# One matmul pair for both parts of the meta tokens, and the second half's factor row one unit earlier, in a hybrid attention and mLSTM encoder layer

## The chip, the cores and the metric

The kernel runs on one core of one Trainium2 chip. The metric is the device time of one execution in microseconds, taken over several runs; the median is compared. The kernel before was run three times: 2815.20, 2803.92 and 2798.67 us, median 2803.92 us.

## What is computed

One encoder layer is applied to two sequences, a prompt of 1024 tokens and a sample of 2048 tokens, each preceded by the same 16 learned "meta" tokens. Everything is in fp32.

```python
def _encoder_layer(h, g_pre, w_in, b_in, na_rpb, ml_conv_w, ml_head_g, w_a, w_b, w_out, g_post):
    xn = _rmsnorm(h, g_pre)
    proj = xn @ w_in + b_in
    na_q, na_k, na_v, na_z, ml_qk, ml_v, ml_z, ml_o, ml_g, mg = jnp.split(proj, SPLIT_IDX, axis=-1)
    ya = _neighbourhood_attention(na_q, na_k, na_v, na_rpb)
    ya = (ya * jax.nn.silu(na_z)) @ w_a
    yb = (_mlstm_branch(ml_qk, ml_v, ml_g, ml_o, ml_conv_w, ml_head_g) * jax.nn.silu(ml_z)) @ w_b
    ga, gb = jnp.split(jax.nn.sigmoid(mg), 2, axis=-1)
    y = (ga * ya + gb * yb) @ w_out
    return h + _rmsnorm(y, g_post)
```

`D_MODEL` is 1024 and the combined projection `w_in` has 6672 columns. The meta tokens take part in both mixers (their keys and values are seen by every attention query, and the mLSTM starts with them) and are dropped at the end.

## The kernel before, in words

**Split products.** Every operand of a large product is held as two parts, a high part in the rounded fp32r format and a low part that is the rest (`xh` and `xl` for the tokens, `whi` and `wlo` for the weights). A product is three matmuls added up in one PSUM bank: high by high, high by low, low by high. The product low by low is left out.

**Two streams.** `dense` is a Python generator that issues the projections and the closing products; `sparse` issues the two mixers. `run` takes from both in turns, by estimated TensorE costs that each `yield` hands over, so the order on TensorE is written out by hand. On the other engines and on SyncE, whose queue starts nearly all transfers, a planner orders the instructions by a simulated timeline.

**The dense stream.** `PLAN` lists groups of columns for pieces of 1024 tokens, which are treated as two halves of 512. The first group, (0, 0, "m"), is the mLSTM part for the whole prompt, the second, (0, 0, "n"), the attention part. Only these two compute the meta tokens, once for both sequences. While the first group runs, the sparse stream has nothing to do yet; the second runs beside the mLSTM of the prompt.

**Jobs of a group.** `layout` makes jobs of two kinds. A feature-major job ("fm", `fm_half`) has four units; a unit is 128 columns of the weights, as stationary operand, by 512 tokens (or two times 264, with the meta tokens, in the first half). A token-major job ("tm", `tm_unit`) has the tokens as the stationary operand, 128 at a time, and 256 or 264 weight columns as the moving operand; over the eight slices of the contraction that is 24 matmuls for each 128 tokens. The first group is one fm job, six tm jobs and a second fm job.

**The meta tokens in a tm job.** They are an entry of their own in the list `todo` (`tok` is None, 16 stationary columns). The order in a job is four times 128 tokens of the first half, then the meta tokens, then four times 128 of the second half. Five tm jobs have such an entry: the one with the columns from 4360 on (gates, 264 wide), two of the mLSTM values, and two of the attention values (256 wide). Each is 24 matmuls with 16 stationary columns (L590 to L592), one evacuation (L601: multiply by the token's norm factor `rc`, add the bias) and two small stores.

**PSUM.** There are three banks under the tag `pj`, two under `tr`, one under `sc`, two under `sm`. tm jobs use `pj` alone, so an entry needs the bank that was filled three entries earlier.

**The norm factor of the prompt.** For the prompt, `x` is not multiplied by its RMS factor ahead of the product; the factor is multiplied in at evacuation. In fm units it has to lie along the free axis, so `rrows` (L317 to L321) makes a row of it: a diagonal matrix times ones on TensorE (tag `sm`), copied by ScalarE into `rr`. Until `rr` exists, the first units of a half cannot be evacuated. `group` therefore gives the units banks from the list `("pj", "pj", "pj", "tr", "tr", "sc")` and collects their evacuations in `late`. When unit `lu` is done with its third quarter (`q == 2`), the function in `self.rwait` issues the row product; after unit `lu`, all evacuations collected are issued. `lu` is 2 in the first half, where a unit takes two banks, and 3, the last unit of the job, in the second half. After that job comes the first tm job, on `pj`.

**The opening.** `opening` loads the first tokens and weights, makes their high and low parts (ScalarE and VectorE by turns), and the factors of the first 512 tokens and of the meta tokens. The pool `xp`, on the right side of SBUF, holds its temporary tiles and is closed when the second half's row is issued; the pools of the mixers take that room afterwards.

**A chain across the group.** The gate columns of the tm job with 264 columns go to DRAM (`gg`, L627 and L629) and are read back as `g_t` (L956, L957) by the prompt's mLSTM, whose first instructions on ScalarE and VectorE are L965 and L966.

Of the kernel before, what the change touches and what calls it, by code (L numbers as in the profile page):

```python
# [9 lines left out]
F32 = mybir.dt.float32  # L10
F32R = mybir.dt.float32r
I32 = mybir.dt.int32
AF = mybir.ActivationFunctionType
ALU = mybir.AluOpType
# [3 lines left out]
P = 128  # L18
# [102 lines left out]
class K:  # L121
# [231 lines left out]
    def opening(self, xp):  # L353

        nc, wp, cp = self.nc, self.wp, self.cp
        self.gpre = cp.tile([P, KT], F32, name="gpre")
        nc.sync.dma_start(self.gpre, self.i["g_pre"])
        nc.vector.tensor_scalar(self.gpre, self.gpre, -0.125, None, op0=ALU.mult)
        xm = cp.tile([P, KT, NM], F32, name="xm")
        nc.sync.dma_start(xm, self.i["xm"].rearrange("p (k t) -> p k t", k=KT))  # L360
        xts = [self.xtload(0, 0, 0, xp, 9)]
        self.wload(1)
        xts += [self.xtload(0, 0, e, xp, 9) for e in (1, 2, 3)]
        self.wload(2)
        mt = xp.tile([P, D], F32, name="xr", bufs=9)
        nc.sync.dma_start(mt[:NM], self.i["meta"])
        toks = self.tokens(0, 0, (0, 1), xp, 9)
        self.wload(3)
        toks += self.tokens(0, 0, (2, 3), xp, 9)
        self.setup2()  # L370
        self.xnext = [self.xtload(0, 512, e, wp, 4) for e in (0, 1)]
        self.wload(4)
        self.xnext += [self.xtload(0, 512, e, wp, 4) for e in (2, 3)]
        self.toks = self.tokens(0, 512, range(4), xp, 9)
        x = self.xparts()
        self.xs.append(tuple(x))
        g = self.gpre.rearrange("p (k a) -> p k a", a=1).to_broadcast([P, KT, NM])
        nc.vector.tensor_tensor(xm, xm, g, op=ALU.mult)
        nc.scalar.activation(x[0][:, :, :NM], xm, AF.Copy)
        nc.vector.tensor_tensor(x[1][:, :, :NM], xm, x[0][:, :, :NM].bitcast(F32), op=ALU.subtract)  # L380
        for e in range(4):
            self.xsplit(x, xts[e], e, NM, self.gpre)
            if e == 0:
                self.wpump(1, 4)
        self.wpump(2, 2)
        self.wpump(3, 2, nc.vector.tensor_copy)
        res = []
        for _ in self.rsum(toks, res, (mt, NM)):
            pass
        self.rc = cp.tile([P, 9], F32, name="rc")  # L390
        self.rr = wp.tile([P, 2, 512], F32, name="rr", tag="gain", bufs=1)
        self.rm = cp.tile([P, NM], F32, name="rm")
        dt = wp.tile([P, HALF], F32, name="dt", tag="thT", bufs=1)
        dg, dm = self.rdiag(res[0], dt), dt[:NM, 512:]
        nc.vector.tensor_scalar(dm, self.ident[:NM, :NM], res[0][:NM, 4:5], None, op0=ALU.mult)
        nc.vector.tensor_copy(self.rc[:, 0:4], res[0][:, 0:4])
        nc.vector.tensor_copy(self.rc[:, 8:9], res[0][:, 4:5])
        self.wpump()
        self.wrp = wp, 2

        def rows():
            self.rrows(dg, self.rr[:, 0], "sm")
            p = self.psum("sm", [P, 512])
            nc.tensor.matmul(p[:, :NM], self.ones[:NM], dm, start=True, stop=True)
            nc.scalar.activation(self.rm, p[:, :NM], AF.Copy)
        self.rwait[0, 0] = rows
# [163 lines left out]
    def tm_unit(self, col, halves, wd):  # L570
        nc, wp = self.nc, self.wp
        ws = self.wtake(2)
        bb = wp.tile([P, WU], F32, name="bb", bufs=2)
        nc.sync.dma_start(bb[:, :wd], _bc(self.i["b_in"], col, wd))
        todo = []
        for x, s, t0, meta in halves:
            base = NM if meta else 0
            todo += [(x, s, base + 2 * P * j, P, 2, t0 + 2 * P * j) for j in range(2)]
            if meta and not (C_MZ <= col < C_GA - wd):
                todo.append((x, s, 0, NM, 1, None))  # L580
        for j, (x, s, c, n, cnt, tok) in enumerate(todo):
            st = wp.tile([P, 2, WU], F32, name="stT", bufs=4)
            for a in range(cnt):
                p = self.psum("pj", [P, 512])
                o = p[:n, :wd]
                xs = slice(c + a * P, c + a * P + n)
                for k in range(KT):
                    wh, wl = ws[k // 4][0][:, k % 4, :], ws[k // 4][1][:, k % 4, :]
                    xh, xl = x[0][:, k, xs], x[1][:, k, xs]
                    nc.tensor.matmul(o, xh, wh, start=k == 0, stop=False)  # L590
                    nc.tensor.matmul(o, xh, wl, start=False, stop=False)  # L591
                    nc.tensor.matmul(o, xl, wh, start=False, stop=k == KT - 1)  # L592
                    if k == 3:
                        if j == len(todo) - 1 and a == cnt - 1:
                            self.wdone()
                        yield 12 * C256
                if j == len(todo) - 1 and a == cnt - 1:
                    self.wdone()
                if s == 0:
                    r = 8 if tok is None else tok // P + a  # L600
                    nc.vector.scalar_tensor_tensor(st[:n, a, :wd], p[:n, :wd], self.rc[:n, r:r + 1], bb[:n, :wd], op0=ALU.mult, op1=ALU.add)  # L601
                else:
                    nc.vector.tensor_tensor(st[:n, a, :wd], p[:n, :wd], bb[:n, :wd], op=ALU.add)
                if a == cnt - 1:
                    self.tm_store(col, wd, s, n, cnt, tok, st)
                yield 12 * C256

    def tm_store(self, col, wd, s, n, cnt, tok, st):
        nc, wp = self.nc, self.wp
# [81 lines left out]
    def group(self, s, t0, meta, cols, reuse, nxt):  # L691
# [4 lines left out]
        for j, (kind, c) in enumerate(jobs):  # L696
            if kind == "tm":
                for cost in self.tm_unit(c[0], [(x,) + h for x, h in zip(self.xs, todo)], c[1]):
                    yield cost
                    self.beside()  # L700
                continue
            ws = self.wtake(len(c))
            last = j == len(jobs) - 1
            for hf in range(2):
                side = None
                if j == 0 and hf == 0 and not reuse:
                    side = self.spread(self.build_half(*todo[1][:2], self.xs), 15)
                elif last and nxt and nxt[0] == "f":
                    side = self.spread(self.ystart(*nxt[1:]), 15) if hf else None
                elif last and nxt:  # L710
                    if hf == 0:
                        nres = []
                        nb = self.build_half(*nxt[:2], nres)
                        side = self.spread(nb, 15, "scaled")
                    else:
                        side = self.spread(nb, 15)
                late = tags = None
                if todo[hf][:2] in self.rwait:
                    late = []
                    tags = iter(("pj", "pj", "pj", "tr", "tr", "sc"))  # L720
                    lu = 3 if hf else 2
                for u, (col, w) in enumerate(zip(c, ws)):
                    for q, cost in enumerate(self.fm_half(col, w, self.xs[hf], *todo[hf], done=self.wdone if hf else None, tags=tags, late=late)):
                        yield cost
                        if side:
                            side()
                        if self.fout:
                            next(self.fout, None)
                        self.beside()
                        if late is not None and u == lu and q == 2:  # L730
                            self.rwait[todo[hf][:2]]()
                    if late is not None and u == lu:
                        for evac in late:
                            evac()
                        late = tags = None
                        del self.rwait[todo[hf][:2]]
                if side:
                    side(True)
# [918 lines left out]
    def dense(self, ctx):  # L1657

        tc, nc = self.tc, self.nc
        self.wp = ctx.enter_context(tc.tile_pool(name="wp", bufs=1, reuse_waits="tile"))  # L1660
        self.requests()
        self.xp = ExitStack()
        xp = self.xp.enter_context(tc.tile_pool(name="xp", bufs=1, side="right", reuse_waits="tile"))
        self.wrp = xp, 4
# [23 lines left out]
    def sparse(self):  # L1688

        for kind, s, rts in STEPS:  # L1690
            if kind == "ml":
                for t0 in range(0, SEQLEN[s], 1024):
                    yield ("m", s, t0)
                yield from self.ml(s)
            else:
                types = _row_types(SEQLEN[s] // 64)
                for t0 in range(0, SEQLEN[s], 1024):
                    if any((types[b][1] + types[b][2]) * 64 > t0 for b in rts):
# [79 lines left out]
```

## Time and profile before

| | |
|---|---|
| median of three runs | 2803.92 us |
| lowest, highest | 2798.67, 2815.20 us |
| the profiled execution's own time | 2802.44 us |
| its span, first to last instruction | 2800.7 us |
| mean granted TensorE clock | 0.998 |
| VectorE, ScalarE busy | 65%, 47% of the span |
| HBM traffic | 233 GB/s over the span |

The profile's page gives the busy time of each engine, the chain of work that ended last, and groups of instructions with the tile they write and read, their count, busy time, mean duration, and the idle time of the engine ahead of them with what ended it. Matmuls are pipelined: one that is listed with 0.28 us is followed by the next after about 0.12 us, so durations of matmuls overlap and a sum of them is not a time. Spacing, from start to start, is what the engine spends. PE is the matmul side of TensorE, PEld its loading of stationary operands, DVE is VectorE, ACT is ScalarE, POOL is GpSimd, SPq is the queue of SyncE.

### The profile page before, as it was taken

Reading aid. Unit: us, or ns where it says so; the run is one execution under the profiler, and the core shown is the slowest. Engines: PE = TensorE matmul, PEld = TensorE weight load, DVE = VectorE, ACT = ScalarE, POOL = GpSimd, SP = SyncE. Lnnn points to the kernel's source line nnn. Section 1 sums busy time; section 2 is a strip of 40 time slices with the busy share of each in tenths; the row PEclk is TensorE's granted clock in tenths of the full one; section 3 lists DMA queues with packets and bytes.
Section 4 is the critical chain, followed back from the end, with each engine's and each line's share of the span. In section 5 each row is a group of like instructions: output and inputs, shape, how many; then the busy total and the mean of one; then the engine's idle time right before and its main releaser. Section 6 shows DMA issues by size and latency. Waiting matters only on the chain.

```text
span 2800.7 us, 48806 instructions
## 1 busy us (share of the span) xinstructions
PE 2766.8 (99%) x17120; PEld 2461.0 (88%) x17120; DVE 1827.2 (65%) x5075; ACT 1313.6 (47%) x3183; POOL 16.2 (1%) x103
## 2 busy tenths in 40 slices
PE   9999999999999999999999999999999999999998
PEld 7998898999899988988888888878887989889898
DVE  5232688676556655456768666575669888797954
ACT  5122556444444444355456555463455645545421
POOL 0000000000000000000000000000000000000000
PEclk9999999999999999999999999999999999999999
DMA  9555768755965554685666786565569898998965
GB/s 369 182 184 196 257 201 315 266 182 176 351 206 176 174 156 142 195 284 167 190 207 207 235 285 216 182 204 170 179 214 349 299 332 255 321 276 279 323 241 212
DMA packets 378278, 655.10 MB, mean 234 GB/s; under 512 B 50896, under 2 KB 199840, under 8 KB 378032
## 3 DMA queue, kind: packets, MB, share of 16 engines
q1 hardware_dynamic: 376912, 649.29, 70.2%
q0 software_dynamic: 1120, 2.69, 0.4%
q8 instruction: 135, 2.21, 0.3%
q14 instruction: 111, 0.91, 0.1%
HBM read 449.61 MB, written 202.22 MB: 233 GB/s over the span
## 4 chain that ended last, share of the span: by engine, by line
PE 88%; DMA 6%; DVE 4%; ACT 1%; issue 1%; SPq 0%; DVEq 0%; ACTq 0%
PE pj L169 15%; PE pj L170 15%; PE pj L171 15%; PE pj L590 7%; PE pj L591 7%; PE pj L592 7%; PE pj L1568 3%; PE sm L923 3%; PE pj L1570 3%; PE pj L1569 3%; PE tr L908 3%; DMA um<-ud 2%; DMA wlo<-wl 1%; PE sm L171 1%; PE sm L170 1%
## 5 line engine op out<-in xcount | busy, mean ns | idle before, releaser
L169 PE MATMUL pj<-xh,whi 128*128 128x512 f32 (+1 forms) x1792 | 705.4, 394 | 1.6 <-ACT whi L263 1.2
L170 PE MATMUL pj<-xl,whi 128*128 128x512 f32 (+1 forms) x1792 | 689.7, 385 | 0.1
L171 PE MATMUL pj<-xh,wlo 128*128 128x512 f32 (+1 forms) x1792 | 688.2, 384 | 0.2 <-DVE wlo L264 0.2
L590 PE MATMUL pj<-whi,xh 128*128 128x256 f32 (+3 forms) x1576 | 450.0, 286 | 1.5 <-ACT st L520 1.5
L591 PE MATMUL pj<-wlo,xh 128*128 128x256 f32 (+3 forms) x1576 | 444.4, 282 | 0.9 <-DMA wlo<-wl 0.9
L592 PE MATMUL pj<-whi,xl 128*128 128x256 f32 (+3 forms) x1576 | 444.3, 282 | 0.0
L171 PEld LDWEIGHTS pj<-xh,wlo 128*128 128x128 f32 x1792 | 337.2, 188 | 71.7 <-DVE wlo L264 0.4
L169 PEld LDWEIGHTS pj<-xh,whi 128*128 128x128 f32 x1792 | 337.2, 188 | 61.9 <-ACT whi L263 2.0
L170 PEld LDWEIGHTS pj<-xl,whi 128*128 128x128 f32 x1792 | 337.7, 188 | 57.3 <-issue 1.0
L590 PEld LDWEIGHTS pj<-whi,xh 128*128 128x128 f32 (+1 forms) x1576 | 294.3, 187 | 3.4 <-ACT st L520 1.9
L591 PEld LDWEIGHTS pj<-wlo,xh 128*128 128x128 f32 (+1 forms) x1576 | 293.9, 186 | 2.1 <-DMA wlo<-wl 1.1
L592 PEld LDWEIGHTS pj<-whi,xl 128*128 128x128 f32 (+1 forms) x1576 | 293.8, 186 | 0.9
L1568 PE MATMUL pj<-whi,mh 128*128 128x256 f32 x768 | 220.5, 287 | 3.1 <-DMA whi<-wh 3.1
L1570 PE MATMUL pj<-whi,mlo 128*128 128x256 f32 x768 | 216.5, 282 | 0.0
L1569 PE MATMUL pj<-wlo,mh 128*128 128x256 f32 x768 | 216.3, 282 | 0.0
L915 DVE TENSOR_TENSOR pts<-tr,pts 96x512 fp32r<-96x512 f32 (+2 forms) x192 | 131.8, 687 | 93.0 <-ACT pts L910 92.3
L910 ACT ACTIVATE pts<-tr 96x512 fp32r<-96x512 f32 (+2 forms) x192 | 113.9, 593 | 134.7 <-PE tr L908 134.4
L169 PE MATMUL pj<-yh,whi 128*128 128x512 f32 x384 | 154.5, 402 | 0.0
L171 PE MATMUL pj<-yh,wlo 128*128 128x512 f32 x384 | 151.3, 394 | 0.0
L170 PE MATMUL pj<-yl,whi 128*128 128x512 f32 x384 | 151.0, 393 | 0.0
L1568 PEld LDWEIGHTS pj<-whi,mh 128*128 128x128 f32 x768 | 145.3, 189 | 5.5 <-DMA whi<-wh 4.0
L1569 PEld LDWEIGHTS pj<-wlo,mh 128*128 128x128 f32 x768 | 145.5, 189 | 1.6
(283 smaller groups left out, 4991.4 us busy)
## 6 DMA issues: line engine op xcount, KB each, us to landing
whi<-wh SPq DMA_DIRECT2D x176, 512.0 KB
wlo<-wl SPq DMA_DIRECT2D x176, 512.0 KB
wraw<-wu SPq DMA_DIRECT2D x64, 512.0 KB
wh<-whi SPq DMA_DIRECT2D x64, 512.0 KB
wl<-wlo SPq DMA_DIRECT2D x64, 512.0 KB
gt<-st SPq DMA_DIRECT2D x96, 256.0 KB
tg<-gt SPq DMA_DIRECT2D x96, 256.0 KB
xt<-xt SPq DMA_DIRECT2D x32, 512.0 KB
```

The source lines that it names most:

```text
L169: mm(out, ah, bh, start=start, stop=False)
L170: mm(out, ah, bl, start=False, stop=False)
L171: mm(out, al, bh, start=False, stop=stop)
L590: nc.tensor.matmul(o, xh, wh, start=k == 0, stop=False)
L591: nc.tensor.matmul(o, xh, wl, start=False, stop=False)
L592: nc.tensor.matmul(o, xl, wh, start=False, stop=k == KT - 1)
L908: nc.tensor.transpose(pt[:ks, ch, :], pr_[:, ch * ks:(ch + 1) * ks], self.ident)
L910: nc.scalar.activation(pts[:ks, :, 0, :], pt[:ks], AF.Copy)
L915: self.nc.vector.tensor_tensor(pts[:ks, :, 1, :], pt[:ks], pts[:ks, :, 0, :].bitcast(F32), op=ALU.subtract)
L1568: nc.tensor.matmul(o, mh[:, k, xs], wh, start=k == 0, stop=False)
L1569: nc.tensor.matmul(o, mh[:, k, xs], wl, start=False, stop=False)
L1570: nc.tensor.matmul(o, ml[:, k, xs], wh, start=False, stop=k == KT - 1)
```

## The change

Four things are changed.

1. A tile `xmp` of 48 columns for each of the eight slices holds the meta tokens' high part in columns 0 to 15, zeros in 16 to 31, and the low part in columns 32 to 47. It is filled in the opening by one memset on GpSimd and two copies on VectorE, in a pool of its own that is closed ahead of the prompt's attention.
2. In the five tm entries of the meta tokens the stationary operand is `xmp`: two matmuls for each slice in place of three, 16 in place of 24. The output has 48 rows; rows 0 to 15 and rows 32 to 47 must be added. ScalarE copies rows 32 to 47 to SBUF, VectorE adds rows 0 to 15, and a second VectorE instruction multiplies by the factor and adds the bias. The product low by low is now included for these tokens. The cost that such an entry hands to `run` falls from twice 12 to twice 8 matmuls.
3. In the second half, the row product is issued after the last quarter of unit 2 (before: after the third quarter of unit 3), and the evacuations of units 0 to 2 directly behind it.
4. Unit 3 of that half takes one bank under `tr` and is evacuated by itself.

```diff
+        nc.gpsimd.memset(self.xmp[:, :, NM:2 * NM].bitcast(F32), 0.0)
+        for a in range(2):
+            nc.vector.tensor_copy(self.xmp[:, :, 2 * NM * a:2 * NM * a + NM], x[a][:, :, :NM].bitcast(F32))
...
-                o = p[:n, :wd]
+                o = p[:3 * NM if tok is None else n, :wd]
...
-                    xh, xl = x[0][:, k, xs], x[1][:, k, xs]
-                    nc.tensor.matmul(o, xh, wh, start=k == 0, stop=False)
-                    nc.tensor.matmul(o, xh, wl, start=False, stop=False)
-                    nc.tensor.matmul(o, xl, wh, start=False, stop=k == KT - 1)
+                    if tok is None:
+                        both = self.xmp[:, k]
+                        nc.tensor.matmul(o, both, wh, start=k == 0, stop=False)
+                        nc.tensor.matmul(o, both, wl, start=False, stop=k == KT - 1)
+                    else:
+                        xh, xl = x[0][:, k, xs], x[1][:, k, xs]
+                        nc.tensor.matmul(o, xh, wh, start=k == 0, stop=False)
+                        nc.tensor.matmul(o, xh, wl, start=False, stop=False)
+                        nc.tensor.matmul(o, xl, wh, start=False, stop=k == KT - 1)
                     if k == 3:
...
-                        yield 12 * C256
+                        yield (8 if tok is None else 12) * C256
...
-                if s == 0:
-                    r = 8 if tok is None else tok // P + a
+                if tok is None:
+                    nc.scalar.activation(st[:n, 1, :wd], p[2 * NM:2 * NM + n, :wd], AF.Copy)
+                    nc.vector.tensor_tensor(st[:n, 1, :wd], p[:n, :wd], st[:n, 1, :wd], op=ALU.add)
+                    nc.vector.scalar_tensor_tensor(st[:n, 0, :wd], st[:n, 1, :wd], self.rc[:n, 8:9], bb[:n, :wd], op0=ALU.mult, op1=ALU.add)
+                elif s == 0:
+                    r = tok // P + a
...
-                yield 12 * C256
+                yield (8 if tok is None else 12) * C256
...
-                    lu = 3 if hf else 2
...
-                        if late is not None and u == lu and q == 2:
+                        if late is not None and u == 2 and q == 2 + hf:
                             self.rwait[todo[hf][:2]]()
-                    if late is not None and u == lu:
+                    if late is not None and u == 2:
                         for evac in late:
                             evac()
-                        late = tags = None
+                        late = None
+                        tags = iter(("tr",)) if hf else None
                         del self.rwait[todo[hf][:2]]
...
+        self.mpool = ExitStack()
+        mpool = self.mpool.enter_context(tc.tile_pool(name="mm", bufs=1, side="right", reuse_waits="tile"))
+        self.xmp = mpool.tile([P, KT, 48], F32R, name="xmp")
...
+                self.mpool.close()
```

## The prediction

> **What bounds the kernel now.** I read the head of the page first, then the busy time by stretches of 70 us, then the waits of TensorE.
>
> ```profile
> span 2800.7 us, 48806 instructions
> PE 2766.8 (99%) x17120; PEld 2461.0 (88%) x17120; DVE 1827.2 (65%) x5075; ACT 1313.6 (47%) x3183; POOL 16.2 (1%) x103
> PE 88%; DMA 6%; DVE 4%; ACT 1%; issue 1%; SPq 0%; DVEq 0%; ACTq 0%
> ```
> ```profile
> core 0: us, PE busy (x) PEld busy (x) DVE busy (x) ACT busy (x) POOL busy (x), PEclk, DMA share, GB/s
> 0.00:70.00 70.00, 65.53 (x392) 55.62 (x393) 35.49 (x91) 38.13 (x68) 1.20 (x18) 1.00 0.97 369
> 70.00:140.00 70.00, 70.00 (x585) 68.87 (x584) 20.29 (x38) 12.95 (x18) 0.00 (x0) 1.00 0.55 182
> 350.00:420.00 70.00, 70.00 (x562) 67.32 (x562) 58.21 (x193) 36.72 (x100) 0.30 (x3) 1.00 0.62 200
> 2100.00:2170.00 70.00, 66.38 (x333) 54.85 (x332) 65.66 (x138) 39.28 (x77) 0.51 (x1) 0.98 1.03 349
> ```
>
> TensorE sets the time: 99% busy, 88% of the chain. In 70 to 140 us (token-major jobs alone) and 350 to 420 us (the same beside the prompt's mLSTM) it has no idle time, so a matmul less there is its spacing less at the end. Idle PE lies in few places; here the waits of TensorE that matter.
>
> ```profile
> PE sc L1320 <- DVE q L1275: 4.9, 5, 1.6
> PE pj L1568 <- DMA whi<-wh: 3.1, 3, 1.5
> ...
> PE sm L877 <- DVE yg L938: 2.0, 1, 2.0
> ...
> PE pj L590 <- ACT st L520: 1.5, 1, 1.5
> ```
>
> No single wait is longer than 2.0 us (columns: sum, count, longest). The last is one wait of 1.5 us for ScalarE's evacuations, at the first token-major job. The change touches it directly.
>
> **Part 1: two matmuls for three.** Five entries of eight slices lose one matmul each: 40 fewer, 32 of 256 columns and 8 of 264. The meta entry of the gates job and of the first values job, first matmul and the first one behind each:
>
> ```profile
> 94.59 0.28 PE L590 MATMUL pj<-whi,xh 128*16 128x264 f32 x1
> ...
> 97.49 0.28 PE L590 MATMUL pj<-whi,xh 128*128 128x264 f32 x1
> ```
> ```profile
> 120.54 0.28 PE L590 MATMUL pj<-whi,xh 128*16 128x256 f32 x1
> ...
> 123.30 0.28 PE L590 MATMUL pj<-whi,xh 128*128 128x256 f32 x1
> 123.42 0.28 PE L591 MATMUL pj<-wlo,xh 128*128 128x256 f32 x1
> ```
>
> 24 matmuls of 264 take 97.49 - 94.59 = 2.90 us, 0.121 each; 24 of 256 take 2.76 us, 0.115 each. The listed 0.28 us is latency that overlaps; charging it (40 x 0.28 = 11.2 us) would be wrong. The sum is 8 x 0.121 + 32 x 0.115 = 4.65 us. The bounds are 4.6 (all at 0.115) and 4.84 (all at 0.121).
>
> Would 48 stationary columns be dearer than 16? The loads of both widths:
>
> ```profile
> L590 PEld LDWEIGHTS pj<-whi,xh 128*128 128x128 f32 x384 | 72.4, 188 | 2.0 <-ACT st L520 1.9
> L590 PEld LDWEIGHTS pj<-whi,xh 128*16 128x16 f32 x24 | 2.3, 94 | 0.5
> ```
>
> A load of 128 columns takes 188 ns against 94 for 16, yet the spacing is the same within 0.005 us on either side of 123.30 (0.115 ahead, 0.12 behind), so 48 lies between two widths that both hide: 0.
>
> By the Trainium skill ("TensorE: Matmul & The Clock Gate", section "Back-to-back issue gap") a warm matmul costs N/2.4 + 2.5 ns, 109 ns for 256 columns and 112.5 for 264, which would make the saving an estimated 4.4 us; the rows above show 115 and 121 ns, and the rows decide.
>
> **Part 2: the longer evacuation.** One VectorE instruction becomes a ScalarE copy and two VectorE instructions. This adds a wait: VectorE's add stands behind ScalarE's copy, and everything later in VectorE's queue behind that. The place where it could bite is the first values job, whose meta entry falls together with the landing of the gates:
>
> ```profile
> 118.23 0.37 SPq L957 DMA_DIRECT2D g_t<-gg  x1
> 123.21 0.36 ACT L965 ACTIVATE g_e<-g_t 128x36 f32<-128x36 f32 x2 [11.81 <-DMA g_t<-gg]
> 123.22 0.29 DVE L966 TENSOR_SCALAR g_lf<-g_t 128x36 f32<-128x36 f32 x2 [1.99 <-DMA g_t<-gg]
> 124.28 0.47 DVE L601 SCALAR_TENSOR_TENSOR stT<-pj,rc,bb 16x256 f32<-16x256 f32 x1
> 359.12 0.38 ACT L1323 ACTIVATE s<-sc 128x256 f32<-128x256 f32 x1
> ```
>
> ScalarE waits 11.81 us for `g_t`, and in the changed order its copy of the meta rows stands behind that wait. Everything ahead moves 2.6 us forward (0.97 from the gates job, 1.69 from part 3). If the transfer moves along, it lands at 120.6; if not, at 123.2. Then come 0.36 for the two gate instructions, some 0.4 for the copy (the row of 128x256 from PSUM), and 0.5 for the add: 121.9 to 124.5. The meta entry itself ends at 123.4 - 2.6 - 0.9 = 119.9, and its bank is wanted two entries later, 2 x 24 x 0.118 = 5.7 us on, at 125.6. Slack of 1.1 to 3.7 us: 0. In the other four entries no DMA stands ahead on either queue; five copies of 0.4 us and five adds of 0.5 us lie beside a TensorE that is full, with ACT at 13 to 37 and DVE at 20 to 58 of 70 us. With that cover gone each would cost its 0.9 us, 4.5 in all; I take 0. The stores are as many as before and move past no queue.
>
> **Part 3: the row one unit sooner.** The end of the second half's job:
>
> ```profile
> 51.12 0.40 PE L169 MATMUL tr<-xh,whi 128*128 128x512 f32 x1
> 51.35 0.39 PE L170 MATMUL tr<-xl,whi 128*128 128x512 f32 x1
> ...
> 55.29 1.02 PE L320 MATMUL sm<-xr,ones 128*128 128x512 f32 x2
> ...
> 57.31 0.40 PE L171 MATMUL tr<-xh,wlo 128*128 128x512 f32 x1
> 59.23 0.39 PE L590 MATMUL pj<-whi,xh 128*128 128x264 f32 x1 [1.51 <-ACT st L520]
> ```
> ```profile
> 46.52 0.68 ACT L312 ACTIVATE xr<-ident,nwy 128x128 f32<-128x128 f32 x2
> 51.09 1.09 ACT L263 ACTIVATE whi<-wraw 128x1056 fp32r<-128x1056 f32 x1 [3.90 <-PE pj L170]
> 56.35 0.60 ACT L321 ACTIVATE rr<-sm 128x512 f32<-128x512 f32 x1 [4.17 <-PE sm L320]
> 58.50 1.83 ACT L520 ACTIVATE st<-pj,bfm 128x512 f32<-128x512 f32 x3
> 52.21 1.26 DVE L264 TENSOR_TENSOR wlo<-wraw,whi 128x1056 fp32r<-128x1056 f32 x1 [4.30 <-ACT whi L263]
> 56.98 1.90 DVE L508 TENSOR_TENSOR pj<-pj,rr 128x512 f32<-128x512 f32 x3 [3.52 <-ACT rr L321]
> ```
>
> The last matmul starts at 57.31 and the next could at 57.54 (spacing 0.23 for 512); it starts at 59.23: 1.69 us lost, because row, `rr`, three multiplications and ScalarE's first evacuation follow one another only from 55.29 on. In the changed order the row is issued at 51.12. Its diagonal is ready at 46.52 + 0.68 = 47.2, so nothing waits for it. ScalarE has one weight cast ahead (to 52.2), `rr` is there at 52.8; VectorE finishes that weight's low part at 53.5 and three multiplications at 55.4; ScalarE's third evacuation ends at about 56.0. TensorE, with the row (1.1 us, paid before too) and unit 3, arrives at 57.5: slack 1.5 us. Only unit 3's bank under `tr`, which no token-major job wants, is evacuated later. Gain 1.69; its bounds are 0 (some wait takes its place) and 1.69.
>
> **Part 4: filling `xmp`.** In the changed order both copies stand on VectorE between these two:
>
> ```profile
> 4.90 0.29 DVE L380 TENSOR_TENSOR xl<-xm,xh 128x128 fp32r<-128x128 f32 x1 [0.38 <-ACT xh L379]
> 6.76 1.42 DVE L335 SCALAR_TENSOR_TENSOR xl<-xt,gpre,xh 128x512 fp32r<-128x512 f32 x2 [1.56 <-ACT xh L334]
> ```
>
> Two copies of 128 elements at no more than 0.29 us end at 5.8, inside the idle time up to 6.76: 0. Were ScalarE's cast early, they would cost 0.6. GpSimd's memset stands in an engine busy for 1.20 of the first 70 us: 0.
>
> **The sum:** 4.65 + 1.69 = 6.34 us. The profiled execution took 2802.44 us, 1.74 more than its span; less 6.34 that is 2796.1. The median of the runs, 2803.92, lies 1.5 above it, so 2797.6 for a median.
>
> **What the sum can't hold.** With the cheaper entries the turns between the streams shift by a few matmuls, and the planned order on VectorE, ScalarE and SyncE changes by up to some 20 places all through the program. That moves stalls elsewhere. The worst stretch now:
>
> ```profile
> 1345.00:1350.00 5.00, 2.81 (x22) 2.41 (x20) 3.34 (x13) 2.89 (x9) 0.00 (x0) 0.99 0.93 330
> 1350.00:1355.00 5.00, 3.46 (x15) 3.27 (x16) 4.49 (x16) 3.24 (x10) 0.00 (x0) 0.50 0.58 165
> 1355.00:1360.00 5.00, 5.00 (x38) 5.00 (x38) 2.17 (x8) 2.07 (x8) 0.00 (x0) 0.83 0.86 270
> ```
>
> PE idles 2.19 + 1.54 = 3.7 us, and the granted clock of 0.50 and 0.83 costs another 1.7 + 0.85: 6.3 us for one such stretch, at the sample's mLSTM.
>
> **The rivals.**
> - *As summed:* 2797.6, own range 2792 to 2804, from the scatter of the three runs (5 below, 11 above their median). Chance 0.48.
> - *The reshuffle also removes that stretch:* 2797.6 - 6.3 = 2791.3. For it: it hangs on short waits in a row that any earlier instruction may break. Against it: the turns hardly shift there. 0.22.
> - *The reshuffle adds such stretches, slower than before:* the same chain, one or two steps of the mLSTM earlier, each of which already waits for VectorE (five waits, 4.9 us). One stretch cancels the gain; from the second on the kernel is slower, 2797.6 + 2 x 6.3 = 2810.2. Against it: nothing in the change adds work there. 0.12.
> - *Paid back to the transfers:* in 2100 to 2170 the DMA engines are full (1.03, 349 GB/s) and PE idles 3.6 us; if that stage is paced by its transfers, coming earlier only means waiting longer, 2802. Against it: its loads start when buffers come free, which moves with PE. 0.10.
> - *The row's step doesn't do what it says,* a different wait taking its place: 2797.6 + 1.7 = 2799.3. 0.08.
>
> The Trainium skill (same page, section "The HAM clock gate (the "warmup" mystery)") has the clock halve after an idle window of about 3.4 us; here no single wait reaches that and the clock still fell, so by the trace a row of short waits is enough.
>
> **How the numbers follow.** The forecast is the likeliest case, 2797.6. The range reaches from 2788 (the second case with the runs' scatter) to 2810 (the third case). A measurement here tells about 0.5%, 14 us, from no change. Faster by more, below 2789.9, comes from about 0.4 of the second case and 0.08 of the first: 0.13, say 0.14. Slower by more, above 2817.9, from a third of the third and stray runs: 0.06. Within: 0.80.
>
> **What would show it.** Right: the wait of L590 on ScalarE at 59 us gone, the first token-major job starting at about 57.5; meta entries of 16 matmuls 0.115 to 0.121 apart; the first-values copy without a PE gap behind it; PE busy lower by some 5 us. Wrong: a wait on `pj` behind a meta entry, spacing above 0.125 with 48 columns, or the sum of PE waits after 1190 us more than 5 us off.

## The result, and the profile after

| | before | after |
|---|---|---|
| median of 12 runs | 2803.48 us | 2794.32 us |
| lowest, highest | 2798.67, 2815.20 | 2791.47, 2798.48 |
| ratio of the runs, 95% interval | | 0.9972 (0.9962 to 0.9982) |
| span of the profiled execution | 2800.7 us | 2794.1 us |

The ratio is 7.8 us less, 5.0 to 10.7 by its interval; the two profiled spans differ by 6.6 us, the two medians by 9.2. The forecast was 6.34 us less, a median of 2797.6 in a range of 2788 to 2810; 2794.32 lies in that range. The prediction gave 0.80 to a change of less than 0.5%, and it is 0.28%. It is still clear of no change: the prediction thought that 14 us were needed for that, and 7.8 are enough. The head of the page after, busy us, share and instructions of each engine:

```profile
span 2794.1 us, 48759 instructions
PE 2762.9 (99%) x17080; PEld 2458.5 (88%) x17080; DVE 1828.9 (65%) x5082; ACT 1316.2 (47%) x3188; POOL 16.7 (1%) x104
```

40 matmuls fewer, TensorE still 99% busy: it sets the time as it did before. The end of the second half's job, TensorE in order of time (start, us, operation):

```profile
51.18 1.02 PE L320 MATMUL sm<-xr,ones 128*128 128x512 f32 x2
51.63 0.79 PE L169 MATMUL tr<-xh,whi 128*128 128x512 f32 x1
...
57.39 0.39 PE L171 MATMUL tr<-xh,wlo 128*128 128x512 f32 x1
57.62 0.28 PE L598 MATMUL pj<-whi,xh 128*128 128x264 f32 x1
```

No bracket with a wait stands behind L598 any more, and it starts 0.23 us after its predecessor: the hole of 1.7 us is closed. On the two engines that were late:

```profile
51.15 1.08 ACT L263 ACTIVATE whi<-wraw 128x1056 fp32r<-128x1056 f32 x1 [3.89 <-PE pj L170]
52.23 0.60 ACT L321 ACTIVATE rr<-sm 128x512 f32<-128x512 f32 x1
54.16 1.88 ACT L523 ACTIVATE st<-pj,bfm 128x512 f32<-128x512 f32 x3 [1.33 <-DVE pj L511]
```
```profile
52.26 1.26 DVE L264 TENSOR_TENSOR wlo<-wraw,whi 128x1056 fp32r<-128x1056 f32 x1 [4.30 <-ACT whi L263]
53.44 1.89 DVE L511 TENSOR_TENSOR pj<-pj,rr 128x512 f32<-128x512 f32 x3
```

The third evacuation ends at 54.16 + 1.88 = 56.0, 1.6 us ahead of L598. The meta entries, all 40 slices by form (ns min/median/max), and the first matmul of the first values entry with the one behind the entry:

```profile
L594 PEld LDWEIGHTS pj<-whi,xmp x40: 120/121/125, 92.8 to 392.0; 128*48 128x48 f32 x40
```
```profile
117.87 0.28 PE L594 MATMUL pj<-whi,xmp 128*48 128x256 f32 x1
...
119.76 0.28 PE L598 MATMUL pj<-whi,xh 128*128 128x256 f32 x1
```

16 matmuls in 1.89 us, 0.118 each: the entry took 2.76 us before. Its evacuation beside the landing of the gates, on ScalarE and VectorE:

```profile
120.40 0.35 ACT L977 ACTIVATE g_e<-g_t 128x36 f32<-128x36 f32 x2 [11.68 <-DMA g_t<-gg]
120.66 0.36 ACT L608 ACTIVATE stT<-pj 16x256 f32<-16x256 f32 x1
```
```profile
121.05 0.41 DVE L609 TENSOR_TENSOR stT<-pj,stT 16x256 f32<-16x256 f32 x1 [0.35 <-ACT stT L608]
```

ScalarE's copy does stand behind the wait for `g_t`. The bank is free at 121.05 + 0.41 = 121.5; TensorE wants it two entries behind 119.76, at 125.4. Between 60 and 420 us the profile has one wait of TensorE, on another bank (sum, count, longest); the kernel before has the same one:

```profile
PE sm L1057 <- DVE g_eT L1059: 0.3, 1, 0.3
```

**Where the time went.** For the same matmul in both traces (meta entries and row products left out of the count), the difference of the start times is the lead; minus is earlier. With the cost left at 12 (e1, e4 and e12) these matmuls stand in the order of the kernel before, one for one. With the cost of 8 the two streams take other turns, so behind 420 us some matmuls move against others; the table gives there the mean over all matmuls within 8 us of the place, and for these kernels it is good to about 2 us.

| at (us of the kernel before) | 57 | 71 | 152 | 419 | 832 | 1371 | 1832 | 2139 | 2459 |
|---|---|---|---|---|---|---|---|---|---|
| after | +0.1 | -1.7 | -4.5 | -6.2 | -2.7 | -13.6 | -6.3 | -10.3 | -7.5 |
| after, run again (e8) | +0.1 | -1.7 | -4.5 | -6.1 | -3.1 | -13.0 | -5.9 | -9.8 | -4.7 |
| row alone (e1) | -0.3 | -2.0 | -2.0 | -1.9 | -2.5 | -3.1 | -2.7 | +1.9 | +4.1 |
| pair alone, cost 8 (e2) | +0.2 | +0.2 | -2.6 | -3.9 | -0.9 | -11.4 | -4.1 | -7.8 | -3.6 |
| cost alone (e3) | -0.2 | -0.2 | -0.2 | +0.7 | +4.3 | -5.3 | +5.4 | +3.2 | +6.1 |
| pair and row, cost 12 (e4) | 0.0 | -1.8 | -4.5 | -5.4 | -4.2 | -3.3 | -2.2 | -3.8 | -2.3 |
| row alone, cost 8 (e11) | -0.1 | -1.9 | -1.9 | -1.7 | +0.9 | -9.5 | -1.5 | -7.6 | -4.1 |
| pair alone, cost 12 (e12) | -0.1 | -0.1 | -2.8 | -4.9 | -6.3 | -8.0 | -8.1 | -11.0 | -6.6 |

The kernels with the cost of 8 all have one order among themselves, so against e3, the cost alone, the lead can be read one for one to the end:

| at (us of e3) | 57 | 71 | 152 | 419 | 832 | 1371 | 1832 | 2139 | 2459 |
|---|---|---|---|---|---|---|---|---|---|
| after | +0.3 | -1.5 | -4.3 | -6.9 | -7.0 | -8.2 | -12.8 | -13.5 | -13.6 |
| pair alone, cost 8 (e2) | +0.4 | +0.5 | -2.3 | -4.7 | -5.3 | -6.1 | -9.3 | -11.0 | -9.7 |
| row alone, cost 8 (e11) | +0.1 | -1.6 | -1.6 | -2.5 | -3.4 | -4.2 | -6.6 | -10.9 | -10.2 |

Up to 420 us the lead grows by the row's 1.8 us, the gates' 1.0 and 0.9 for each values entry, and these steps are the same in every kernel that has the part. Behind 420 us the lead over the kernel before swings by some 10 us. Against e3, whose order is the same, these swings are gone, so they come from the order of the turns. What is left there is a drift of several us, and part of that is the one execution that each trace shows: e3's was 5.7 us above its own median, and e11's 1.2 below. The stretch that was the worst before, in the profile after (columns: stretch, length, then busy us of PE, PEld, DVE, ACT, POOL, and the granted clock):

```profile
1345.00:1350.00 5.00, 5.00 (x45) 5.00 (x44) 2.28 (x11) 1.80 (x6) 0.00 (x0) 1.00 0.22 61
1350.00:1355.00 5.00, 5.00 (x45) 5.00 (x44) 3.99 (x19) 1.38 (x3) 0.00 (x0) 1.00 0.39 107
```

It is gone, 5.00 us of PE at full clock. But the waits of TensorE in 1420 to 1840 us, of which before had one of 0.4 us, are now

```profile
PE sc L1332 <- DVE q L1287: 3.8, 4, 2.0
PE sm L170 <- DVE v L1313: 1.6, 2, 1.2
PE tr L170 <- DVE ccl L1324: 0.9, 1, 0.9
```

### The profile page after: what moved, and what is told of

The parts are those of the page before. It is cut to its first block, busy times and chain, and to the rows that moved or that the text cites. A ratio compares the mean times of both kernels' runs of the same rounds, so it can differ in the third digit from the quotient of the medians.

```text
span 2794.1 us, 48759 instructions
## 1 busy us (share of the span) xinstructions
PE 2762.9 (99%) x17080; PEld 2458.5 (88%) x17080; DVE 1828.9 (65%) x5082; ACT 1316.2 (47%) x3188; POOL 16.7 (1%) x104
## 4 chain that ended last, share of the span: by engine, by line
PE 81%; DMA 10%; DVE 6%; ACT 1%; issue 1%; SPq 0%; DVEq 0%; ACTq 0%
PE pj L169 14%; PE pj L170 14%; PE pj L171 14%; PE pj L598 6%; PE pj L599 6%; PE pj L600 6%; PE sm L935 3%; PE pj L1582 3%; PE pj L1580 3%; PE pj L1581 3%; DMA um<-ud 3%; PE tr L920 2%; DMA tg<-gt 1%; DMA wlo<-wl 1%; DMA kr<-nk 1%
## 5 line engine op out<-in xcount | busy, mean ns | idle before, releaser
L598 PE MATMUL pj<-whi,xh 128*128 128x256 f32 (+1 forms) x1536 | 439.1, 286 | 1.2 <-DMA whi<-wh 1.2
L599 PE MATMUL pj<-wlo,xh 128*128 128x256 f32 (+1 forms) x1536 | 432.6, 282 | 0.9 <-DMA wlo<-wl 0.9
L600 PE MATMUL pj<-whi,xl 128*128 128x256 f32 (+1 forms) x1536 | 432.6, 282 | 0.0
L598 PEld LDWEIGHTS pj<-whi,xh 128*128 128x128 f32 x1536 | 289.6, 189 | 2.0 <-DMA whi<-wh 1.5
L599 PEld LDWEIGHTS pj<-wlo,xh 128*128 128x128 f32 x1536 | 289.4, 188 | 1.3 <-DMA wlo<-wl 1.1
L600 PEld LDWEIGHTS pj<-whi,xl 128*128 128x128 f32 x1536 | 289.4, 188 | 0.0
```

## The experiments

Two theories. The first: what counts is the TensorE time taken out in the first 420 us (4.65 + 1.69 us), and the swings behind it come from the new order of the engines and add up to little. The second: the new order, above all the stretch at 1345 us, carries a good part of the gain. Parts were taken alone, then doses were added. Three things can be set apart: the pair (two matmuls for three), the row (one unit sooner), and the cost handed to the turns (8 or 12).

**e1, the row alone.**

```diff
 (kernel before)
-                    lu = 3 if hf else 2
-                        if late is not None and u == lu and q == 2:
+                        if late is not None and u == 2 and q == 2 + hf:
-                    if late is not None and u == lu:
+                    if late is not None and u == 2:
-                        late = tags = None
+                        late = None
+                        tags = iter(("tr",)) if hf else None
```

> Only the row product one unit sooner; three matmuls for the meta tokens as before. If the gain is TensorE time taken out where it was seen: the wait of 1.5 us at 59 us gone, the first token-major job at 57.6, 1.7 us less than the kernel before (ratio 0.9994), the lead of 1.7 us standing at 420 us. If the new order of the other engines is what carries the gain of the changed kernel: anything from 8 us less to 5 us more, with a lead at 420 us that has nothing to do with the end.

Measured: 1.0002 (0.9994 to 1.0011). The first job starts at 57.29 and the lead of 1.8 us stands until 2018 us (-2.5 there). Then it is lost, in a place that the edit does not touch; the waits of TensorE there (2080 to 2180 us; sum, count, longest), of before and of e1:

```profile
PE sm L877 <- DVE yg L938: 2.0, 1, 2.0
PE sm L923 <- ACT prb L891: 1.6, 1, 1.6
```
```profile
PE sm L923 <- ACT prb L891: 3.3, 1, 3.3
PE sm L877 <- DVE yg L938: 2.0, 1, 2.0
```

One wait for ScalarE is 1.7 us longer, and in 2115 to 2140 us the granted clock is 0.86 in place of 1.00; another 2 us go between 2139 and 2459. This execution took 2806.56 us, 2.7 above the kernel's own median, so its trace can't explain the median. The row alone did not show its 1.7 us at the end; its interval just reaches it.

**e2, the pair alone, with the cost of 8.** The changed kernel with `lu = 3 if hf else 2` and the three lines of the row as before.

> Only the two matmuls for three; the row product where it was. If the gain is TensorE time: a lead of 4.4 to 4.7 us at 420 us, built in five steps of 0.9 to 1.0, and 4.65 us less in all (ratio 0.9983), the wait at 59 us still there. If the new order carries the gain: the lead at 420 us is the same, but the end differs from it by more than 3 us.

Measured: 0.9980 (0.9971 to 0.9989), 5.6 us less. The lead of the first three entries is 2.8 us (0.96, 0.90, 0.91), and 3.9 at 419 us. The two entries of the attention values lie among the mLSTM's matmuls, where the turns of this kernel differ from those before. Against e3, whose turns are the same, the lead is 4.7 at 419. In e4 and e12, which have the turns of the kernel before, each of these two entries gives 0.91 to 0.92 us. The five steps add up to 4.6. The wait at the first job is still there:

```profile
59.43 0.39 PE L598 MATMUL pj<-whi,xh 128*128 128x264 f32 x1 [1.52 <-ACT st L523]
```

**e3, the cost alone.**

```diff
 (kernel before, both yields of tm_unit)
-                        yield 12 * C256
+                        yield (8 if tok is None else 12) * C256
```

> The kernel before with only the cost handed over for the meta entries lowered from 12 to 8: the same instructions, the turns between the two streams shifted. If the gain is TensorE time: no lead at 420 us and a time within 3 us of the kernel before (ratio 0.999 to 1.001), though single stalls after 420 us move. If the new turns carry a good part of the gain: 2 us less or better, with the stretch of half clock at 1345 us gone.

Measured: 0.9998 (0.9989 to 1.0006). No lead in the first 420 us (a lag of 0.7 at 419), and the same instructions. Yet the stretch at 1345 us is gone here too, and the waits come back in 1420 to 1840 us:

```profile
1345.00:1350.00 5.00, 5.00 (x41) 4.83 (x40) 3.14 (x11) 2.02 (x6) 0.00 (x0) 1.00 0.99 303
1350.00:1355.00 5.00, 5.00 (x45) 5.00 (x44) 3.10 (x12) 2.40 (x7) 0.00 (x0) 1.00 0.80 258
```
```profile
PE sc L1320 <- DVE q L1275: 2.0, 3, 1.4
PE sm L170 <- DVE v L1301: 1.7, 2, 1.2
PE tr L170 <- DVE ccl L1312: 1.7, 2, 1.5
...
```

The lead goes from +4.3 to -5.3 and back to +5.4. So the swing at 1371 us in the changed kernel is the doing of the shifted turns; it is given back by 1832 us, and its net worth is nothing that can be measured.

**e4, pair and row with the cost left at 12.** Both yields of `tm_unit` are `12 * C256` in the changed kernel.

> The changed kernel with the cost of the meta entries left at 12, so that the turns between the streams stay as in the kernel before. If the gain is TensorE time: a lead of 6.0 us at 420 us and 6.3 us less than before (ratio 0.9977), equal to the changed kernel within 2 us. If the new turns carry a part: 2 us or more slower than the changed kernel, with the stretch at 1345 us back.

Measured: 0.9973 (0.9964 to 0.9983), the changed kernel's time, with the stretch still there (PE busy 1.99 of 5 us, from 1345):

```profile
1345.00:1350.00 5.00, 1.99 (x12) 1.44 (x11) 4.96 (x17) 4.31 (x13) 0.00 (x0) 0.96 0.50 181
```

The other kernels with the cost of 12, e1 and e12, have the stretch too (PE busy 1.91 of 5 us from 1345, and 1.15 from 1340), and those with the cost of 8 have not. The second theory asked for at least 2 us lost; 0.3 were, but two such ratios can't be told apart to better than some 4 us. The four couples below, which put the cost at 0.6 us, about 2 either way, are the better evidence; they leave no room for the 6.3 us at which the stretch was priced.

**e5, the copy on VectorE.** `nc.scalar.activation(..., AF.Copy)` becomes `nc.vector.tensor_copy`.

> The changed kernel with the copy of rows 32 to 47 on VectorE in place of ScalarE, so that it never stands behind ScalarE's wait for the gates. If the longer evacuation is hidden, as predicted: the lead at 420 us stays at 5.9 us (within 0.3) and no wait on a pj bank is seen behind a meta entry in either kernel; in all within 3 us of the changed kernel. If ScalarE's place in it costs: the lead at 420 us grows by up to 0.9 us for each of the five entries.

Measured: 0.9970 (0.9957 to 0.9983); the lead is 4.5 us at 152 and 5.9 at 419, and no wait of TensorE follows a meta entry. Where the copy stands makes no difference. That the longer evacuation is hidden rests on this together with TensorE's missing waits after the change.

**e6, 128 stationary columns.** `xmp` is 128 wide, with zeros behind column 48, and the product has 128 rows.

> The changed kernel with 128 stationary columns for the meta tokens, 80 of them zeros behind the low part. If the width of the stationary operand is hidden, as predicted: loads of 188 ns in place of 121, the spacing still 0.115 to 0.121 us, the lead at 420 us 5.9 us, in all within 3 us of the changed kernel. If width costs: spacing above 0.125 us and at least 0.4 us less lead at 420 us.

Measured: 0.9969 (0.9957 to 0.9981); lead 4.6 at 152, 6.3 at 419 us. The loads of this kernel:

```profile
L595 PEld LDWEIGHTS pj<-whi,xmp x40: 187/188/192, 92.6 to 391.9; 128*128 128x128 f32 x40
```

The load is 67 ns longer than with 48 columns. The entries take 1.90 to 1.97 us in place of 1.88 to 1.92, so all but at most 0.1 us an entry of the width is hidden, as read from before.

**e7, the row behind unit 1.**

```diff
 (changed kernel)
-                        if late is not None and u == 2 and q == 2 + hf:
+                        if late is not None and u == 2 - hf and q == 2 + hf:
-                    if late is not None and u == 2:
+                    if late is not None and u == 2 - hf:
-                        tags = iter(("tr",)) if hf else None
+                        tags = iter(("pj", "tr")) if hf else None
```

> The changed kernel with the second half's row product one more unit earlier, behind unit 1. If the limits are as read: the diagonal is ready at 47.2 us and unit 1 ends at 45.6, so TensorE waits some 1.6 us for ScalarE ahead of the row product, and the lead at 71 us is 0.1 us in place of 1.7; the later steps keep their 4.2, so about 1.6 us slower than the changed kernel (ratio 0.9978 against the kernel before). If the diagonal is no limit: the lead at 71 us stays 1.7 us, since the wait at 59 us is already gone.

Measured: the wait is there, 1.53 us for the diagonal, which ends at 47.69:

```profile
47.73 1.13 PE L320 MATMUL sm<-xr,ones 128*128 128x512 f32 x2 [1.53 <-ACT xr L312]
```

The lead at 71 us is a lag of 0.5 (this execution was 0.5 us late from the opening on). The time is 0.9972 (0.9961 to 0.9983): 0.9978 was expected and lies inside, so does no loss at all. One more unit closes no other hole and opens this one. What that costs at the end is not shown: matmul for matmul this kernel is 2.2 us behind the changed one from 71 to 530 us and level with it at 832. Between these two places TensorE waits 0.2 us for weight transfers here, and 2.1 in the changed kernel.

**e8, the changed kernel once more.**

> The changed kernel once more, for a second profile. If the stalls behind 420 us hang on the order of the instructions: they stand in the same places and the lead over the kernel before goes through the same values within 1 us (6 at 420, 3 at 830, 14 at 1370, 5 at 1830, 12 at 2140, 8 at 2460). If they hang on the chance of one execution: the lead differs by several us behind 420.

Measured: one run of 2798.05 us, and the leads in the table. Matmul for matmul, the two executions agree within 0.03 us up to 530 us and within 0.6 at 832, 1371, 1832 and 2139; at 2459 they are 2.8 apart, against 1 that was allowed. The granted clock differs (columns as at 1345 us above), first in the earlier execution, then in this one:

```profile
2430.00:2443.00 13.00, 10.13 (x57) 9.84 (x58) 4.94 (x15) 4.04 (x11) 0.00 (x0) 0.74 1.01 303
```
```profile
2430.00:2443.00 13.00, 9.93 (x49) 8.91 (x50) 4.39 (x11) 2.90 (x9) 0.00 (x0) 0.61 1.05 320
```

0.13 of 13 us is 1.7 us, most of the 2.0 us by which the two part between 2300 and 2459. The places of the swings hang on the order of the instructions, the sizes in part on the execution, so a single trace tells the end to some 3 us at best.

**e9, a dose on the row.** After e1 the question was whether time at 51 us reaches the end at all. The row product is issued 16 times.

```diff
-                self.rrows(dg, self.rr[:, 1], "sm")
+                p = self.psum("sm", [P, 512])
+                for _ in range(16):
+                    nc.tensor.matmul(p, self.ones, dg, start=True, stop=True)
+                nc.scalar.activation(self.rr[:, 1], p, AF.Copy)
```

> The changed kernel with the second half's row product issued 16 times in place of once, a dose of TensorE time in the place where the row's step gains its 1.7 us. Each is two matmuls of 0.23 to 0.43 us, so the dose D is 7 to 13 us; the lead at 71 us shows it. If TensorE time taken out or put in at that place passes to the end: the kernel is slower than the changed one by D within 3 us. If the stages behind it make up for it, as the row alone (ratio 1.0002) and the row behind unit 1 (0.9972) might mean: slower by less than half of D.

```profile
50.78 13.89 PE L454 MATMUL sm<-xr,ones 128*128 128x512 f32 x32
64.11 0.80 PE L169 MATMUL tr<-xh,whi 128*128 128x512 f32 x1
```

From the row's start to the next product are 13.33 us in place of 0.45: a dose of 12.9. Measured: 1.0017 (1.0009 to 1.0026), 0.0045 above the changed kernel, 12.6 us, and by the ends of both intervals 7.6 to 17.9. Matmul for matmul it is 12.5 us behind the changed kernel at 152 us and 15.2 at the end. Time added at that place passes to the end. That time taken out there does so too is not shown by this: another wait could take its place.

**e10, a dose on the pair.** `for k in list(range(KT)) * (3 if tok is None else 1)` in `tm_unit`; the sums start anew each time. The loop also passes its inner `yield` three times, so an entry hands over four times 8 in place of twice 8, and the turns shift as well.

> The changed kernel with the 16 matmuls of each meta entry done three times over (the sums are started anew each time), 160 more matmuls of 0.115 to 0.121 us: a dose of 18.6 us, 7.7 of it beside the prompt's mLSTM. If TensorE time there is the kernel's time: a lead of 5.9 us at 420 us becomes a lag of 12.7, and the kernel is 18.6 us slower than the changed one within 3 us (ratio 1.0038 against the kernel before). If later stages make up for it: less than half of that.

Measured: a lag of 6.8 us at 152 (11.2 us behind the changed kernel, for 96 matmuls of 0.117) and 14.0 at 419; 1.0056 (1.0041 to 1.0072), 0.0084 above the changed kernel, 23.5 us, and by the ends of both intervals 16.5 to 31 (four runs of this kernel). Less than half of the dose is excluded, and 18.6 lies inside. The 3 us that were allowed around it were missed by 2; whether the turns or the scatter gave the rest is open.

**e11 and e12, the last two combinations.** e11 is e1 with the cost of 8; e12 is e2 with the cost of 12.

> The row product one unit sooner and the handed-over cost of 8, with three matmuls for the meta tokens: the row's step alone under the other order of the turns. If the row's step is worth its 1.7 us at the end and the first run of it alone had a dear order: 1.7 us less than the kernel with the cost alone (0.9998), ratio 0.9992. If its gain is lost behind 420 us whatever the order: 0.9998 or above.

> The two matmuls for three with the row where it was and the cost left at 12: the last of the eight combinations of pair, row and cost. If the parts add up: 4.65 us less than the kernel before (ratio 0.9983), and over the four couples of kernels that differ in one part alone the pair is worth 4.65 us, the row 1.7 and the cost 0, each within 1.5. If the parts hang together (the pair of use under one order only): a ratio outside 0.997 to 0.9993.

Measured: e11 0.9991 (0.9983 to 1.0000), 2.0 us below e3 where 1.7 was expected; e12 0.9975 (0.9964 to 0.9986). All eight ratios:

| | row as before, cost 12 | row sooner, cost 12 | row as before, cost 8 | row sooner, cost 8 |
|---|---|---|---|---|
| three matmuls | 1 | 1.0002 | 0.9998 | 0.9991 |
| two matmuls | 0.9975 | 0.9973 | 0.9980 | 0.9972 |

Over the four couples that differ in one part alone, the pair is worth 25, 29, 18 and 19 in units of 0.0001, mean 23 (6.4 us); the row -2, 2, 7 and 8, mean 4 (1.1 us); the cost 2, 11, -5 and 1, mean 2 (0.6 us). Intervals of single ratios are 9 to 11 of these units to either side, so a mean of four couples is uncertain by about 7 (2 us). The pair's 6.4 missed the 1.5 us that e12 allowed around 4.65 by a little, the others kept it; 4.65, 1.69 and 0 all lie within the means' own width. For the row so does nothing at all.

## Why the prediction was right

**Part 1, the pair: right.** Spacing, not the listed duration, was the price. The five entries gave 4.6 us by steps of 0.90 to 0.96 (said: 4.65). At the end the pair is worth 6.4 us, about 2 either way; a charge by listed durations, 11.2 us, lies outside. The spacing of a matmul of 256 columns is 0.118 us with 48 stationary columns where it was 0.115 with 16: 0.05 us an entry that the sum put at nothing.

**Part 2, the longer evacuation: right.** `g_t` moved along and landed at 120.4 (said: 120.6); the bank was free at 121.5 (said: 121.9) with 3.9 us of slack. TensorE waits for no bank behind a meta entry, and e5 shows no price for ScalarE's place.

**Part 3, the row: right at its place, not shown at the end.** ScalarE's third evacuation ends at 56.0 as worked out, and the gain at that place is 1.8 us (said: 1.69). At the end the row is worth 1.1 us, about 2 either way, which can't be told from nothing. e9 shows that time added there arrives, with a dose seven times as large. Why e1 alone showed nothing stays open: its interval just reaches 1.7 us, and e11, with the other turns, gave 2.0.

**Part 4, filling `xmp`: right.** The two copies take 0.22 us each in VectorE's idle time:

```profile
4.25 0.29 DVE L380 TENSOR_TENSOR xl<-xm,xh 128x128 fp32r<-128x128 f32 x1 [0.38 <-ACT xh L379]
4.46 0.22 DVE L402 CAST xmp<-xh 128x128 fp32r<-128x128 f32 x1
4.59 0.22 DVE L402 CAST xmp<-xl 128x128 fp32r<-128x128 f32 x1
6.63 1.41 DVE L335 SCALAR_TENSOR_TENSOR xl<-xt,gpre,xh 128x512 fp32r<-128x512 f32 x2 [1.82 <-ACT xh L334]
```

**The sum.** The measured 7.8 us are 1.5 more than summed, inside the interval of 5.0 to 10.7. Whether that excess is real is open.

**The rivals.** The measured median lies 3.3 us below the forecast of 2797.6 and 3.0 above the second rival's 2791.3, so the time alone does not decide between them. The runs do: e3 lost the stretch at 1345 us and gained nothing that can be measured, e4 and e12 kept it and are within 0.0003 of the changed kernel. The removal of the stretch and the coming of other ones were put up as two cases that exclude each other. Both happened, in one kernel: some 11 us won by 1371 us and 7 given back by 1832, and e3 shows the same with no work taken out. A stretch removed from the middle of this kernel is no gain by itself. Paying back to the transfers did not happen in the changed kernel at the stage that was named (2100 to 2170 us): its lead over the kernel before grows there from 8.0 to 10.8 us, and its lead over e3 stands at 13.5. In e1 and e4 the lead shrinks at that stage, by 2.9 and 2.3 us; there it is a longer wait for ScalarE (3.3 and 2.5 us at the line where before waits 1.6) and a lower clock. What looks like paying back, in the other direction, is e7's 2.2 us between 530 and 832 us, in a single execution. Of the marks, PE busy fell by 3.9 us (said: some 5), and the waits of TensorE behind 1190 us by 3.9.

## What to carry to other kernels

Where an engine is full, price a removed matmul by the spacing of its neighbours in that stretch, and look for the one wait that the moved step closes; both can be summed before anything runs. Here a new order of turns moved stalls by more than the change is worth and gave them back elsewhere, so read the lead right behind the edit, where it is exact, and further on only against a kernel that has the same order. When a small part alone shows nothing, a dose many times its size in the same place tells whether time added there reaches the end; that time taken out does so too has to be shown by taking it out.

## What the runs showed of the hardware that was not expected

A load of the stationary operand is recorded with 94, 121 and 188 ns for 16, 48 and 128 columns: 81 ns and 0.84 for each column. The Trainium skill ("TensorE: Matmul & The Clock Gate", section "LDWEIGHTS (loading the stationary operand)") gives the columns divided by 1.2 in ns, which is 13, 40 and 107: the slope agrees with the trace, the 81 ns are on top. Even loads of 188 ns, one for each matmul, let the matmuls follow one another 0.119 us apart (e6).

The row product of ones by a diagonal, whose operands are plain fp32, costs 12.9 / 15 = 0.86 us for 512 columns (e9), two matmuls of 0.43 in the trace, where a matmul of 512 columns in fp32r takes 0.23.
